# Hybrid SSD and Gated DeltaNet block: sums of squares of k from the diagonal of kq, another order of a unit's last steps, gate loads one ahead, wider quads in the FFN

## The chip, the cores and the metric

The kernel runs on one core of a Trainium2 chip. The metric is the device time of one execution in microseconds (us). TensorE (PE) multiplies, VectorE (DVE), ScalarE (ACT) and GpSimd (POOL) work on tiles, and SyncE (SP) issues the loads.

## The reference

One decoder block on 256 tokens of width 2048: a Mamba-2 mixer (SSD, 8 groups) and a Gated DeltaNet mixer (GDN, 16 qk heads, 32 v heads of 128) side by side, merged by sigmoid gates, then w_o, then a SwiGLU FFN (hidden 5632), with RMS norms and shift, scale and gate from a condition vector. Around the change stand the GDN normalisation and the merge:

```python
q = l2_normalize(q.reshape(bsz, seq, GDN_N_QK_HEADS, Dk)) * (Dk ** -0.5)
k = l2_normalize(k.reshape(bsz, seq, GDN_N_QK_HEADS, Dk))
...
a_mat = jnp.where(strict, jnp.einsum('bhcld,bhcsd->bhcls', kc, kc) * dec * bc[..., None], 0.0)
...
qk = jnp.einsum('bhcld,bhcsd->bhcls', qc, kc) * dec
...
o = rms_norm(o, norm_w) * jax.nn.silu(z.astype(f32).reshape(bsz, seq, H, Dv))
...
merged = jax.nn.sigmoid(gate_ssm) * y_ssm + jax.nn.sigmoid(gate_gdn) * y_gdn
```

l2_normalize divides by the root of the sum of squares plus 1e-6. The products of k with k hold these sums for k on their diagonal.

## The kernel before, in words

All weights are read from HBM once, as items of 512 KB. An item is loaded on SP's queue (L144, tile raw, 5 buffers), split by ScalarE into a rounded part hi (L146) and by VectorE into the rest lo (L148, 4 buffers each), and used by 24 products of 128x256 on TensorE (hi by x hi, hi by x lo, lo by x hi: L221 to L223; the form with two tiles of four blocks, quad_items, L243 to L245). pump() (L155) takes one item: it loads ahead up to LA + 1 = 4 items, issues the products, runs what is due behind earlier ones (posts), and then advances a generator by one step. A generator yields how many pumps go by until its next step, times a pace (RG for the GDN units, R_S for the SSM groups). So the mixing work is strung between the weight items, and every engine works off its instructions in the order in which pump() wrote them. SP's queue too is in order: a load that waits holds back those behind it.

The GDN mixer is eight units hu of 4 v heads and 2 qk heads, gdn_mix(hu) (L715), whose 256 tokens are two chunks c of 128. At its end a unit already works on the next one's head (gdn_head, L647): seg_rhs and seg_exp (L573, L580) for the decays E; squares (L666) and ssq (L673, one-column products with ones) for the sums of squares of q and k; rsqrt (L200 to L206, two operations on VectorE and twelve on GpSimd) to r8; kq (L686, L688) for k by k and q by k under masks, km and qm; scales for rb and bp on GpSimd (L697); and n_tile (L705) for N = E bp km. Its own steps are then: E times qm (L759), transposes of k and v, QT (transposes of E, L793), an inverse of N by blocks through DRAM (Tp L802, Tm L807, tv L814), v0, S and o0 (L864 to L880), ks and qs (L887, L893), v1 (L925), o1 (L934), norm of o (var L908 to L910 and rsqrt), gated (fo L916, o L919) and emit (the transposes ot, L943, and yh, yl). PSUM has three banks for the items' sums (plin) and five (pmx) that all tiles of the mixing steps share in turn.

Each unit's output goes through its projection w_gp, whose result proj_items adds to accg (L591). After the last unit gate_g_post (L977) multiplies accg by a gate, which was stored in DRAM and is loaded again as ggt (gg_load, L973, two buffers), in eight blocks pr, two ahead: that is the handover to the SSM groups. In the FFN the inputs h2h and h2l are made in 16 tiles (L1264 to L1267), and after tiles 4, 8 and 12 (t = 5, 9, 13) three items run, one for each of the three first accumulators, which so far need four tiles more each time.

Of the kernel before, what the change touches and what calls it, by code (L numbers as in the profile page):

```python
# [37 lines left out]
RG = [1.0] * 7 + [0.9]  # L38
# [7 lines left out]
DG = [0] + [1] * 7  # L46
# [28 lines left out]
def block_kernel(ctx: ExitStack, tc: tile.TileContext, xT, cvec, vec, dskip, consts,  # L75
# [154 lines left out]
    def quad_items(src, n, xh, xl, done, sync=False):  # L230
        bank_of = {}

        def mk(q, j):
            def mm(hi, lo):
                ah, al = xh(), xl()
                if q == 0:
                    bank_of[j] = plin.tile([P, 2, S], F32, tag="lin", name="ps_lin")
# [410 lines left out]
    def gdn_head(hu, unit):  # L648
# [7 lines left out]
        def seg_in(c):  # L656
            rhs.append(seg_rhs(gp, sl, c, 96 + h0, ("T", "T") if c == 0 else ("N", "N")))
# [5 lines left out]
        def squares():  # L663
            for i in range(2):
                sq.append(gp.tile([P, 2, S], F32, tag="T", name="sq", bufs=2))
                A.activation(sq[i], unit["qkv"][:, 2 * i:2 * i + 2, :], AF.Square)  # L666

        def ssq():
            bs_ = bank("ssq")
            for j in range(4):  # L670
                for c in range(2):
                    i = c * 4 + j
                    T_.matmul(bs_[:, 0, i:i + 1], sq[j // 2][:, j % 2, CS[c]], ones[:, 0:1], start=True, stop=True)  # L673
            a8 = gsm.tile([P, 8], F32, tag="a8", name="a8")
            V.tensor_scalar(a8, bs_[:, 0, 0:8], EPS, None, ADD)
            hd["r8"] = rsqrt(gsm, a8, 8, "r8")

        def kq():
            qT, kT = unit["qkv"][:, 0:2, :], unit["qkv"][:, 2:4, :]
            for c in range(2):  # L680
# [4 lines left out]
                km.append(gp.tile([P, 2, P], F32, tag="W", name="km", bufs=2))  # L685
                V.tensor_tensor(km[c], b[:, 0:2, :], mid(nsl, 2), MUL)  # L686
# [26 lines left out]
        return seg_in, seg_out, squares, ssq, kq, scales, n_tile, store  # L713

    def gdn_mix(hu, units):  # L715
        unit = units[hu]
        nxt = units[hu + 1] if hu + 1 < NHU else None
        if hu == 0:
# [4 lines left out]
            seg_in, seg_out, squares, ssq, kq, scales, n_tile, store = gdn_head(hu, unit)  # L723
            seg_in(0)
            yield 1
            seg_out(0)
            seg_in(1)
            yield 1
            squares()
            seg_out(1)  # L730
            kq()
            yield 1
            ssq()
# [14 lines left out]
        nx = gdn_head(hu + 1, nxt) if nxt is not None else [lambda *a: None] * 8  # L748
        seg_in, seg_out, squares, ssq, kq, scales, n_tile, store = nx
# [32 lines left out]
        for j in range(1, 15):  # L782
# [5 lines left out]
            G.tensor_tensor(G3[:, j + 1:16, 0:j], G3[:, j + 1:16, 0:j], t3, ADD)  # L788
        QT = []
# [7 lines left out]
        yield Y_SUB[hu]  # L797
# [72 lines left out]
        A.copy(v0, b)  # L870
        seg_in(0)
# [11 lines left out]
        seg_out(0)  # L883
# [29 lines left out]
        def gated(c, ro):  # L913
# [4 lines left out]
            for h in range(4):  # L918
                V.scalar_tensor_tensor(o[c][:, h, :], o[c][:, h, :], fo[:, h:h + 1],  # L919
                                       zs[:, c, h * P:h * P + P], MUL, MUL)  # L920
        square(0)
        yield 1
# [6 lines left out]
        squares()  # L929
        seg_in(1)  # L930
# [6 lines left out]
        seg_out(1)  # L937
# [9 lines left out]
        gated(0, ro0)  # L947
        ro1 = norm(1)
        ssq()
        yield 1  # L950
        emit(0)
        kq()
        yield 1
        gated(1, ro1)
        scales()
# [21 lines left out]
    def gate_g_post(pr):  # L977
        def f(ps):
            dst = accg[:, 2 * pr:2 * pr + 2, :]
            V.scalar_tensor_tensor(dst, gg_of[pr], 1.0, dst, ADD, MUL)  # L980
            if pr + 2 < 8:
                gg_load(pr + 2)
        return [f]
# [119 lines left out]
    for g in range(NG):  # L1103
        gens.append((ssm_mix(g, unit[NHU + g]), mark + DS, R_S if g < 7 else 1.0))
        if g + 1 < NG:
            gg = [lambda: None] * 5 + [lambda: gg_load(0), lambda: gg_load(1), lambda: None]
# [124 lines left out]
    quad_items(w_gu, 3, lambda: F_["h"], lambda: F_["l"], ffn_post)  # L1231
    for j in range(3, FT):
# [17 lines left out]
    with tc.tile_pool(name="ff", bufs=1) as ff:  # L1250
# [7 lines left out]
        for t in range(KT + 1):  # L1258
            if t in (5, 9, 13):
                for _ in range(3):  # L1260
# [32 lines left out]
def _layout(inp):  # L1293
# [65 lines left out]
    def qtiles(w):  # L1359
        wq = w[:, :768].reshape(4, 4, P, 3, 2, P).transpose(3, 0, 2, 4, 1, 5).reshape(3, 4, P, 1024)  # L1360
        return np.concatenate([wq, tiles(w[:, 768:]).reshape(-1, 4, P, 1024)])

    a["w_o"] = qtiles(f["w_o"][0])
    gu = f["w_gate_up"][0].reshape(D, 2, FT, P).transpose(0, 2, 1, 3).reshape(D, 2 * FT * P)
    a["w_gu"] = qtiles(gu)
# [26 lines left out]
```

## Time and profile before

| what | us |
|---|---|
| median of 3 runs | 2792.67 (2792.53 to 2794.1) |
| the profiled execution | 2796.09 |
| its span | 2794.3 |
| TensorE busy | 2681.2 (96%) |
| VectorE busy | 1884.6 (67%) |
| ScalarE busy | 1370.3 (49%) |
| GpSimd busy | 308.1 (11%) |

The mean granted clock of TensorE is 0.985 of full speed. The GDN units run from about 270 to 1290, the handover to the SSM from about 1290 to 1345, the FFN from about 2045. A busy share is a mean over stages; what a stage is limited by is read from its own stretch.

### The profile page before, as it was taken

What the parts mean: (1) busy time and instruction counts of PE and PEld (TensorE: products, weight loads), DVE (VectorE), ACT (ScalarE), POOL (GpSimd) and SP (SyncE); (2) the same over time, 40 slices, a digit from 0 to 9 for tenths busy, and PEclk for the clock granted to TensorE, in tenths of its full rate; (3) what the DMA queues carried; (4) which work ended last, traced back from release to release, by engine and by line L of the source; (5) the groups of instructions that cost most, each with busy time, mean ns of one, the idle gap of its engine ahead of it and who ended that gap; (6) DMA issues with size and microseconds to landing.
All of it is one profiled execution on the core that took longest, in us unless ns stands there. A gap on an engine that the chain in (4) does not pass through costs nothing.

```text
span 2794.3 us, 51759 instructions
## 1 busy us (share of the span) xinstructions
PE 2681.2 (96%) x20930; PEld 2550.3 (91%) x20930; DVE 1884.6 (67%) x2794; ACT 1370.3 (49%) x2250; POOL 308.1 (11%) x684
## 2 busy tenths in 40 slices
PE   6999999999999999998899999999989999999998
PEld 5988898999899998897799989999989999999997
DVE  7777657668587686766667767677666666655444
ACT  3335554655455555454565565664444444444442
POOL 0000312403123041310000000002100000000000
PEclk8999999999999999998899999999999999999999
DMA  8886647556474664743555544546656666655553
GB/s 331 317 313 212 199 161 242 177 197 227 145 251 158 215 201 165 237 144 127 189 185 193 172 160 159 174 166 238 239 173 227 226 226 226 228 200 196 194 195 130
DMA packets 183283, 566.90 MB, mean 203 GB/s; under 512 B 34753, under 2 KB 43777, under 8 KB 183041
## 3 DMA queue, kind: packets, MB, share of 16 engines
q1 hardware_dynamic: 154306, 552.56, 57.9%
q10 hardware_dynamic: 28736, 11.01, 1.5%
q8 instruction: 164, 2.69, 0.4%
q14 instruction: 77, 0.63, 0.1%
HBM read 552.49 MB, written 11.01 MB: 202 GB/s over the span
## 4 chain that ended last, share of the span: by engine, by line
PE 65%; issue 15%; DVE 7%; ACT 5%; POOL 4%; DMA 4%; SPq 0%; ACTq 0%; DVEq 0%; POOLq 0%
PE ps_lin L221 14%; PE ps_lin L223 14%; PE ps_lin L222 14%; PE ps_z L267 3%; PE ps_z L269 3%; PE ps_z L268 3%; DVE lo L148 2%; ACT hi L146 2%; DMA araw<-in_w_ada 1%; DMA raw<-in_w_g 1%; PE td L837 1%; PE tw L829 1%; PE ps_q L405 1%; DVE araw L333 1%; PE ps_lin L245 1%
## 5 line engine op out<-in xcount | busy, mean ns | idle before, releaser
L148 DVE TENSOR_TENSOR lo<-raw,hi 128x1024 fp32r<-128x1024 f32 x825 | 1014.3, 1234 | 723.4 <-ACT hi L146 721.5
L146 ACT CAST hi<-raw 128x1024 fp32r<-128x1024 f32 x825 | 860.5, 1050 | 597.2 <-PE ps_lin L222 287.3
L221 PE MATMUL ps_lin<-hh,hi 128*128 128x256 f32 x1792 | 509.5, 284 | 6.7 <-DVE accg L591 6.7
L223 PE MATMUL ps_lin<-hh,lo 128*128 128x256 f32 x1792 | 500.8, 279 | 0.6 <-DVE lo L148 0.6
L222 PE MATMUL ps_lin<-hl,hi 128*128 128x256 f32 x1792 | 500.9, 280 | 0.0
L221 PE MATMUL ps_lin<-h2h,hi 128*128 128x256 f32 x1312 | 362.1, 276 | 0.0
L222 PE MATMUL ps_lin<-h2l,hi 128*128 128x256 f32 x1312 | 362.1, 276 | 0.0
L223 PE MATMUL ps_lin<-h2h,lo 128*128 128x256 f32 x1312 | 362.1, 276 | 0.0
L221 PEld LDWEIGHTS ps_lin<-hh,hi 128*128 128x128 f32 x1792 | 340.9, 190 | 10.8 <-issue 9.3
L222 PEld LDWEIGHTS ps_lin<-hl,hi 128*128 128x128 f32 x1792 | 341.8, 191 | 3.6 <-issue 2.4
L223 PEld LDWEIGHTS ps_lin<-hh,lo 128*128 128x128 f32 x1792 | 340.4, 190 | 0.8 <-DVE lo L148 0.8
L221 PE MATMUL ps_lin<-yh,hi 128*128 128x256 f32 x896 | 259.9, 290 | 13.3 <-DVE accg L591 11.9
L222 PE MATMUL ps_lin<-yl,hi 128*128 128x256 f32 x896 | 253.4, 283 | 0.0
L223 PE MATMUL ps_lin<-yh,lo 128*128 128x256 f32 x896 | 253.3, 283 | 0.0
L221 PEld LDWEIGHTS ps_lin<-h2h,hi 128*128 128x128 f32 x1312 | 246.3, 188 | 0.0
L222 PEld LDWEIGHTS ps_lin<-h2l,hi 128*128 128x128 f32 x1312 | 246.3, 188 | 0.0
L223 PEld LDWEIGHTS ps_lin<-h2h,lo 128*128 128x128 f32 x1312 | 246.3, 188 | 0.0
L267 PE MATMUL ps_z<-hi,hh 128*128 128x512 f32 x512 | 207.7, 406 | 0.0
L269 PE MATMUL ps_z<-hi,hl 128*128 128x512 f32 x512 | 201.5, 393 | 0.0
L268 PE MATMUL ps_z<-lo,hh 128*128 128x512 f32 x512 | 200.5, 392 | 0.0
L223 PE MATMUL ps_lin<-fh,lo 128*128 128x256 f32 x704 | 194.3, 276 | 0.0
L221 PE MATMUL ps_lin<-fh,hi 128*128 128x256 f32 x704 | 194.3, 276 | 0.0
(328 smaller groups left out, 5295.6 us busy)
## 6 DMA issues: line engine op xcount, KB each, us to landing
raw<-in_w_gu SPq DMA_DIRECT2D x176, 512.0 KB, 4.2
raw<-in_w_g SPq DMA_DIRECT2D x143, 512.0 KB, 4.4
raw<-in_w_ada SPq DMA_DIRECT2D x128, 512.0 KB, 5.0
raw<-in_w_s SPq DMA_DIRECT2D x96, 512.0 KB, 3.8
raw<-in_w_dn SPq DMA_DIRECT2D x88, 512.0 KB, 4.2
araw<-in_w_ada SPq DMA_DIRECT2D x64, 512.0 KB, 7.6
raw<-in_w_gz SPq DMA_DIRECT2D x64, 512.0 KB, 4.5
raw<-in_w_gp SPq DMA_DIRECT2D x64, 512.0 KB, 4.2
```

The costliest lines, as they stand in the source:

```text
L146: A.copy(hi, raw)
L148: V.tensor_sub(lo, raw, hi.bitcast(F32))
L221: T_.matmul(ps[:, t, :], hi[:, s], h_, start=kt == 0, stop=False)
L222: T_.matmul(ps[:, t, :], hi[:, s], al[:, kt, :], start=False, stop=False)
L223: T_.matmul(ps[:, t, :], lo[:, s], h_, start=False, stop=kt == nk - 1)
L245: T_.matmul(ps[:, t, :], hi[:, s], al[:, kt, :], start=False, stop=False)
L267: T_.matmul(pss[c], hh[:, kt, cs], hi[:, s], start=kt == 0, stop=False)
L268: T_.matmul(pss[c], hh[:, kt, cs], lo[:, s], start=False, stop=False)
L269: T_.matmul(pss[c], hl[:, kt, cs], hi[:, s], start=False, stop=kt == KT - 1)
L333: V.scalar_tensor_tensor(raw, raw, 0.5, cact[:, hs], MUL, MUL, accum_out=ada2[:, j, hf:hf + 1])
L405: T_.matmul(ps[:, t, :], hi[:, s], x1[:, kt, :], start=first, stop=last)
L829: T_.matmul(b[:, h, :], N[c][:, h, :], Vo(c, bs)[:, h], start=True, stop=True)
```

## The change

Four things change.

1. Sums of squares. squares() makes only q's, and ssq() four one-column products instead of eight. For k four scalar_tensor_tensor per unit multiply the k by k tile with the identity and sum the row into the accumulator, which is written to a8. kq is called from ssq, so its products, the diagonals and the masks move from the unit's last steps to the step of S and o0.
2. Order of a unit's last steps. Besides, seg_out(0) and scales go to the step of ks and qs, gated(0) to that of o1, seg_in(1) and seg_out(1) to later ones, and the two transposes QT one pump later with one pump less behind them. Unit 0's generator begins one pump later (DG), unit 7's pace is 0.95 instead of 0.9 (RG).
3. Handover. The load of gate block pr + 1 is issued ahead of the product of block pr, in place of the load of pr + 2 behind it; one load is issued at the start instead of two.
4. FFN. w_gate_up's first six pairs of columns (3 before) are laid out as quads; the last three accumulators come from pmx, and six items run at t = 5, 9 and 13.

```diff
-RG = [1.0] * 7 + [0.9]
+RG = [1.0] * 7 + [0.95]
 R_M = 1.2
...
 NPER = 4
-DG = [0] + [1] * 7
+DG = [1] * 8
 DS = 1
...
                 if q == 0:
-                    bank_of[j] = plin.tile([P, 2, S], F32, tag="lin", name="ps_lin")
+                    bank_of[j] = plin.tile([P, 2, S], F32, tag="lin", name="ps_lin") if j < 3 else \
+                        bank("ps_lin", (P, 2, S))
                 ps = bank_of[j]
...
         def seg_in(c):
-            rhs.append(seg_rhs(gp, sl, c, 96 + h0, ("T", "T") if c == 0 else ("N", "N")))
+            rhs.append(seg_rhs(gp, sl, c, 96 + h0, ("N", "N") if c == 0 else ("T", "T")))
...
         def squares():
-            for i in range(2):
-                sq.append(gp.tile([P, 2, S], F32, tag="T", name="sq", bufs=2))
-                A.activation(sq[i], unit["qkv"][:, 2 * i:2 * i + 2, :], AF.Square)
+            sq.append(gp.tile([P, 2, S], F32, tag="T", name="sq", bufs=2))
+            A.activation(sq[0], unit["qkv"][:, 0:2, :], AF.Square)
         def ssq():
+
             bs_ = bank("ssq")
-            for j in range(4):
+            for j in range(2):
                 for c in range(2):
-                    i = c * 4 + j
-                    T_.matmul(bs_[:, 0, i:i + 1], sq[j // 2][:, j % 2, CS[c]], ones[:, 0:1], start=True, stop=True)
-            a8 = gsm.tile([P, 8], F32, tag="a8", name="a8")
-            V.tensor_scalar(a8, bs_[:, 0, 0:8], EPS, None, ADD)
-            hd["r8"] = rsqrt(gsm, a8, 8, "r8")
-
-        def kq():
+                    T_.matmul(bs_[:, 0, 2 * c + j:2 * c + j + 1], sq[0][:, j, CS[c]], ones[:, 0:1],
+                              start=True, stop=True)
+            a8 = gsm.tile([P, 2, 4], F32, tag="a8", name="a8")
+            kq(a8)
+            V.tensor_scalar(a8[:, :, 0:2], bs_[:, 0, 0:4].rearrange("p (c j) -> p c j", j=2), EPS, None, ADD)
+            V.tensor_scalar(a8[:, :, 2:4], a8[:, :, 2:4], EPS, None, ADD)
+            hd["r8"] = rsqrt(gsm, a8.rearrange("p c j -> p (c j)"), 8, "r8")
+
+        def kq(a8):
             qT, kT = unit["qkv"][:, 0:2, :], unit["qkv"][:, 2:4, :]
...
                 km.append(gp.tile([P, 2, P], F32, tag="W", name="km", bufs=2))
+                for j in range(2):
+                    V.scalar_tensor_tensor(km[c][:, j, :], b[:, j, :], 1.0, ident, MUL, MUL,
+                                           accum_out=a8[:, c, 2 + j:3 + j])
                 V.tensor_tensor(km[c], b[:, 0:2, :], mid(nsl, 2), MUL)
...
             nc.sync.dma_start(pools["i16"], consts[0:64, C_I16:C_I16 + 256])
-            seg_in, seg_out, squares, ssq, kq, scales, n_tile, store = gdn_head(hu, unit)
+            seg_in, seg_out, squares, ssq, scales, n_tile, store = gdn_head(hu, unit)
+            squares()
             seg_in(0)
             yield 1
+            ssq()
             seg_out(0)
+            yield 1
             seg_in(1)
             yield 1
-            squares()
             seg_out(1)
-            kq()
-            yield 1
-            ssq()
             yield 1
...
             G.tensor_tensor(G3[:, j + 1:16, 0:j], G3[:, j + 1:16, 0:j], t3, ADD)
+        yield 1
         QT = []
...
             QT.append(QTc)
-        yield Y_SUB[hu]
+        yield Y_SUB[hu] - 1
         gd = dr.tile([64 * 256], F32, tag="gd", name="gd")
...
         A.copy(v0, b)
+        squares()
         seg_in(0)
...
         A.copy(o[0], b)
-        seg_out(0)
+        ssq()
         yield 1
...
                                        zs[:, c, h * P:h * P + P], MUL, MUL)
+        seg_out(0)
         square(0)
+        scales()
         yield 1
...
         ro0 = norm(0)
-        squares()
-        seg_in(1)
         yield 1
...
         square(1)
-        seg_out(1)
+        gated(0, ro0)
         ogh, ogl = y_tiles(hu)
...
         yield 1
-        gated(0, ro0)
         ro1 = norm(1)
-        ssq()
+        seg_in(1)
         yield 1
         emit(0)
-        kq()
+        seg_out(1)
         yield 1
         gated(1, ro1)
-        scales()
         n_tile(0)
...
         def f(ps):
+            if pr + 1 < 8:
+                gg_load(pr + 1)
             dst = accg[:, 2 * pr:2 * pr + 2, :]
             V.scalar_tensor_tensor(dst, gg_of[pr], 1.0, dst, ADD, MUL)
-            if pr + 2 < 8:
-                gg_load(pr + 2)
         return [f]
...
         if g + 1 < NG:
-            gg = [lambda: None] * 5 + [lambda: gg_load(0), lambda: gg_load(1), lambda: None]
+            gg = [lambda: None] * 6 + [lambda: gg_load(0), lambda: None]
             unit.append(s_in(g + 1, G0 + NHU + g, gg if g == 0 else None))
...
-    quad_items(w_gu, 3, lambda: F_["h"], lambda: F_["l"], ffn_post)
-    for j in range(3, FT):
+    quad_items(w_gu, 6, lambda: F_["h"], lambda: F_["l"], ffn_post)
+    for j in range(6, FT):
         lin_items([w_gu[j, b] for b in range(4)], lambda: F_["h"], lambda: F_["l"], KT, ffn_post(j))
...
             if t in (5, 9, 13):
-                for _ in range(3):
+                for _ in range(6):
                     pump()
...
```

Three places show what moves; rows are in each engine's order of issue.

The end of a GDN unit on VectorE before, in the step with ssq and the next one with kq (a8's row is L675, lo and accg belong to the weight items, yl to the output):

```order
L201 TENSOR_SCALAR roy<-roy 128x4
L675 TENSOR_SCALAR a_8158<-ssq 128x8
L200 TENSOR_SCALAR r8y<-a_8158 128x8
L201 TENSOR_SCALAR r8y<-r8y 128x8
L148 TENSOR_TENSOR lo<-raw,hi 128x1024
L591 TENSOR_TENSOR accg<-ps_lin,accg 128x512
L945 SCALAR_TENSOR_TENSOR yl<-ot,vs,yh 128x4x128
L686 TENSOR_TENSOR km<-kq,cst 128x256
L688 TENSOR_TENSOR qm<-kq,cst 128x256
L686 TENSOR_TENSOR km<-kq,cst 128x256
L688 TENSOR_TENSOR qm<-kq,cst 128x256
```

And VectorE now, in the step of S and o0, some six steps earlier in the unit:

```order
L148 TENSOR_TENSOR lo<-raw,hi 128x1024
L592 TENSOR_TENSOR accg<-ps_lin,accg 128x512
L690 SCALAR_TENSOR_TENSOR km,a_7949<-kq,cst 128x128 x2
L692 TENSOR_TENSOR km<-kq,cst 128x256
L694 TENSOR_TENSOR qm<-kq,cst 128x256
L690 SCALAR_TENSOR_TENSOR km,a_7949<-kq,cst 128x128 x2
L692 TENSOR_TENSOR km<-kq,cst 128x256
L694 TENSOR_TENSOR qm<-kq,cst 128x256
L677 TENSOR_SCALAR a_7949<-ssq 128x2x2
L678 TENSOR_SCALAR a_7949<-a_7949 128x2x2
L200 TENSOR_SCALAR r8y<-a_7949 128x8
L201 TENSOR_SCALAR r8y<-r8y 128x8
```

The four km, qm rows now stand behind vt, with the diagonals (L690, two rows of two) ahead of the masks, and r8's two operations close the group.

VectorE from the step of v1 on before (var and roy are the norm of c = 0, fo and o its gates):

```order
L200 TENSOR_SCALAR roy<-var 128x4
L201 TENSOR_SCALAR roy<-roy 128x4
L148 TENSOR_TENSOR lo<-raw,hi 128x1024
L591 TENSOR_TENSOR accg<-ps_lin,accg 128x512
L935 TENSOR_TENSOR o_7900<-o_8070,o_7900 128x512
L148 TENSOR_TENSOR lo<-raw,hi 128x1024
L591 TENSOR_TENSOR accg<-ps_lin,accg 128x512
L916 SCALAR_TENSOR_TENSOR fo<-roy,rq 128x4
L919 SCALAR_TENSOR_TENSOR o_7899<-o_7899,fo,zs 128x128 x4
```

And now:

```order
L200 TENSOR_SCALAR roy<-var 128x4
L201 TENSOR_SCALAR roy<-roy 128x4
L148 TENSOR_TENSOR lo<-raw,hi 128x1024
L592 TENSOR_TENSOR accg<-ps_lin,accg 128x512
L942 TENSOR_TENSOR o_7942<-o_8152,o_7942 128x512
L923 SCALAR_TENSOR_TENSOR fo<-roy,rq 128x4
L926 SCALAR_TENSOR_TENSOR o_7941<-o_7941,fo,zs 128x128 x4
L148 TENSOR_TENSOR lo<-raw,hi 128x1024
L592 TENSOR_TENSOR accg<-ps_lin,accg 128x512
```

fo and the four products of o stand ahead of a lo and an accg that they stood behind.

SP's queue at the handover before (w_gp is the last unit's projection, w_s the first SSM group's input):

```order
L144 DMA raw<-in_w_gp 128x1024 x2
L975 DMA ggt<-ggd 128x512 x2
L144 DMA raw<-in_w_gp 128x1024 x2
L975 DMA ggt<-ggd 128x512
L144 DMA raw<-in_w_gp 128x1024
L975 DMA ggt<-ggd 128x512
L144 DMA raw<-in_w_gp 128x1024
L975 DMA ggt<-ggd 128x512
L144 DMA raw<-in_w_gp 128x1024
L975 DMA ggt<-ggd 128x512
L144 DMA raw<-in_w_s 128x1024
```

And now:

```order
L144 DMA raw<-in_w_gp 128x1024 x3
L980 DMA ggt<-ggd 128x512
L144 DMA raw<-in_w_gp 128x1024 x2
L980 DMA ggt<-ggd 128x512
L144 DMA raw<-in_w_gp 128x1024
L980 DMA ggt<-ggd 128x512
L144 DMA raw<-in_w_gp 128x1024
L980 DMA ggt<-ggd 128x512
L144 DMA raw<-in_w_gp 128x1024
L980 DMA ggt<-ggd 128x512
L144 DMA raw<-in_w_s 128x1024
```

The first two loads of ggt come apart, and that of block 2, the first that has to wait for a buffer, stands behind six blocks of w_gp instead of four.

## Rows read from the trace of the kernel before

**Rows 1.** Stretches: a unit, and the handover; us, busy by engine, PEclk, DMA, GB/s.

```profile
893.00:1010.00 117.00, 114.12 (x882) 106.47 (x881) 86.10 (x148) 60.42 (x114) 30.40 (x70) 1.00 0.60 199
...
1290.00:1345.00 55.00, 34.47 (x208) 32.87 (x207) 21.95 (x36) 13.18 (x22) 3.72 (x12) 0.77 0.24 82
...
1345.00:1350.00 5.00, 5.00 (x25) 5.00 (x25) 0.86 (x3) 0.00 (x0) 0.00 (x0) 0.50 0.59 202
```

**Rows 2.** TensorE's waits, units 0 to 7 (270 to 1255): total us, times, longest.

```profile
PE qt L793 <- DVE E L759: 11.1, 8, 1.8
PE tv L814 <- DVE Tm L807: 7.1, 3, 3.7
PE ot L943 <- DVE o L919: 7.1, 7, 1.2
PE seg L580 <- ACT T L573: 4.7, 1, 4.7
```

**Rows 3.** Timeline of TensorE at a unit's end: start, us, instruction, [idle before].

```profile
744.51 0.28 PE L221 MATMUL ps_lin<-yh,hi 128*128 128x256 f32 x1
...
747.33 1.84 PE L673 MATMUL ssq<-ones,sq 128*128 128x1 f32 x16
749.04 0.36 PE L221 MATMUL ps_lin<-yh,hi 128*128 128x256 f32 x1
```

**Rows 4.** VectorE's waits, units 0 to 7 (270 to 1255).

```profile
DVE N L705 <- POOL bp L697: 17.8, 8, 3.5
```

**Rows 5.** Timeline of GpSimd in the same steps, first, slowest and last of twelve.

```profile
742.92 0.20 POOL L203 TENSOR_TENSOR rot<-roy 128x4 f32<-128x4 f32 x1 [65.16 <-DVE roy L201]
...
745.18 1.19 POOL L203 TENSOR_TENSOR rot<-roy 128x4 f32<-128x4 f32 x1
...
747.02 0.20 POOL L206 TENSOR_TENSOR roy<-roy,rot 128x4 f32<-128x4 f32 x1
```

**Rows 6.** Timeline of VectorE in the same steps.

```profile
752.70 1.14 DVE L919 SCALAR_TENSOR_TENSOR o<-o,fo,zs 128x128 f32<-128x128 f32 x4
...
754.63 0.16 DVE L675 TENSOR_SCALAR a<-ssq 128x8 f32<-128x8 f32 x1
...
757.54 0.41 DVE L686 TENSOR_TENSOR km<-kq,cst 128x256 f32<-128x256 f32 x1
```

**Rows 7.** TensorE's waits in unit 7 alone (1130 to 1255).

```profile
PE tv L814 <- DVE Tm L807: 1.8, 1, 1.8
```

**Rows 8.** Waits at the handover (1285 to 1350): SP's queue, then TensorE.

```profile
SPq L975 <- DVE accg L980: 52.3, 6, 11.9
...
PE ps_lin L221 <- DVE accg L591: 18.6, 5, 6.7
```

**Rows 9.** Timelines at the handover: VectorE, SP's queue, ScalarE, VectorE, SP's queue.

```profile
1298.72 0.69 DVE L980 SCALAR_TENSOR_TENSOR accg<-ggt,accg 128x512 f32<-128x512 f32 x1
...
1299.44 0.33 SPq L975 DMA_DIRECT2D ggt<-ggd  x1
1299.87 0.37 SPq L144 DMA_DIRECT2D raw<-in_w_gp  x1
...
1304.14 1.04 ACT L146 CAST hi<-raw 128x1024 fp32r<-128x1024 f32 x1 [8.23 <-DMA raw<-in_w_gp]
...
1305.22 1.23 DVE L148 TENSOR_TENSOR lo<-raw,hi 128x1024 fp32r<-128x1024 f32 x1 [5.80 <-ACT hi L146]
1306.36 0.69 DVE L591 TENSOR_TENSOR accg<-ps_lin,accg 128x512 f32<-128x512 f32 x1
...
1307.80 0.33 SPq L975 DMA_DIRECT2D ggt<-ggd  x1
```

**Rows 10.** Groups by line and form: count, busy us, mean ns, idle before.

```profile
L333 DVE DVE_READ_ACCUMULATOR raw<-raw,cact 128x1 f32 x128 | 10.4, 81 | 0.0
```

**Rows 11.** Timelines in the FFN's start: ScalarE, then VectorE.

```profile
2059.93 1.05 ACT L146 CAST hi<-raw 128x1024 fp32r<-128x1024 f32 x1 [1.68 <-PE ps_lin L245]
...
2062.16 0.48 DVE L1264 SCALAR_TENSOR_TENSOR htmp<-accs,wsf,rf 128x256 f32<-128x256 f32 x1
```

More of the change, by code (lines that the diff above doesn't have):

```diff
@@ L712, in store @@
                         .rearrange("h (p s) -> p h s", s=P), hd["N"][c])
-        return seg_in, seg_out, squares, ssq, kq, scales, n_tile, store
+        return seg_in, seg_out, squares, ssq, scales, n_tile, store
     def gdn_mix(hu, units):
@@ L747, in gdn_mix @@
         CS = [slice(0, P), slice(P, S)]
-        nx = gdn_head(hu + 1, nxt) if nxt is not None else [lambda *a: None] * 8
-        seg_in, seg_out, squares, ssq, kq, scales, n_tile, store = nx
+        nx = gdn_head(hu + 1, nxt) if nxt is not None else [lambda *a: None] * 7
+        seg_in, seg_out, squares, ssq, scales, n_tile, store = nx
         eg = ecum[:, 96 + h0:100 + h0]
@@ L1358, in _layout, with qtiles @@
     a["w_sp"] = ptiles(f["w_ssm_proj"][0])
[L1359 to L1363, printed above, removed]
+    def qtiles(w, n):
+        wq = w[:, :256 * n].reshape(4, 4, P, n, 2, P).transpose(3, 0, 2, 4, 1, 5).reshape(n, 4, P, 1024)
+        return np.concatenate([wq, tiles(w[:, 256 * n:]).reshape(-1, 4, P, 1024)])
+    a["w_o"] = qtiles(f["w_o"][0], 3)
     gu = f["w_gate_up"][0].reshape(D, 2, FT, P).transpose(0, 2, 1, 3).reshape(D, 2 * FT * P)
-    a["w_gu"] = qtiles(gu)
+    a["w_gu"] = qtiles(gu, 6)
     wd = f["w_down"][0].reshape(FT, P, 16, P).transpose(2, 0, 1, 3).reshape(8, 11, BLK, P, P)
```

## The prediction, made before the changed kernel ran

> **What bounds the kernel now.** I read the table of stretches first, then TensorE's waits, then the instructions around those waits. In a GDN unit TensorE is busy 114.12 of 117 us while VectorE has 86.10 and ScalarE 60.42 [rows 1]: TensorE sets the pace, and only what takes work or a wait from it counts. The exception is the handover from GDN to SSM: from 1290 to 1345 TensorE is busy 34.47 of 55 us at a granted clock of 0.77, from 1345 to 1350 at 0.50 (the level 1.2 GHz), and no engine is full there [rows 1]. So there are two places to look at: the waits inside the eight units, and the handover.
>
> Inside the units TensorE's waits are few: the QT transposes for the products E (11.1 us in 8 waits, none over 1.8), the transposes tv for Tm (7.1 in 3), the output transposes ot for o (7.1 in 7), and once 4.7 us for seg at the start of unit 0 [rows 2]. An item of weights takes TensorE about 2.8 us (from 744.51 to 747.33 in rows 3): this is what one pump is worth.
>
> **The sum, against the profiled execution (2796.1 us, 3.4 above the median of 2792.67).** A measurement of this kernel can tell about 0.2%, 5.6 us, from no change.
>
> *Sums of squares.* The eight one-column products (16 instructions) hold TensorE from 747.33 to the next item at 749.04, 1.71 us [rows 3]. Half of them go, in 8 units: 8 x 0.85 = **-6.8**. The other end is a gain of nothing, if the wait that stands beside them comes back elsewhere. The Trainium skill (TensorE: Matmul & The Clock Gate, Back-to-back issue gap) gives about 60 cycles at 2.4 GHz, 25 ns, for a product of up to 64 columns; by that figure 64 removed instructions would be worth an estimated 1.6 us. Here 16 took 1.71 us, 107 ns each, and the measured row decides. The eight products of kq are only moved. ScalarE loses one of a unit's two Squares, which is off the path: ScalarE has 57 us idle in a unit.
>
> *QT one pump later.* The four products E run on VectorE behind the four N of the step before; N itself waits on GpSimd for bp, 17.8 us in 8 waits [rows 4]. The extra pump moves the QT transposes 2.8 us later on TensorE, more than the longest wait of 1.8, and with the sums of squares a few steps earlier bp is ready long before N. So the whole wait goes: **-11** (lower end -6, if N, now one step later for c=1, delays E by about what bp's wait did). The pump is taken from the yields behind it, so tv comes at the same item as before.
>
> *Gates of c=0 one pump earlier.* The rsqrt chain of GpSimd runs from 742.92 to 747.22, twelve operations; one beside a lo takes 1.19 us instead of 0.20 [rows 5]. On VectorE the four gate products come at 752.70, behind a lo and an add, and end at 753.84 [rows 6]; a wait of ot is 7.1 / 7 = 1.0 us on average [rows 2], so TensorE was there about 752.8. In the new order they stand right behind the o add of the step before, some 5 us earlier, just about when the chain ends; ssq's time before ot has gone too. I take **-6** of the 7.1; the ends are -7 and 0. By the Trainium skill (SBUF — State Buffer, the section on two separate sides) an operation of VectorE with two SBUF inputs and one of GpSimd that reads SBUF lock each other out for a whole instruction; the 1.19 agrees, and by that rule a second such meeting would put 1 us back into each ot. The margin is a rival below, not a term.
>
> *Pace of unit 7, 0.9 to 0.95.* Its steps spread a little, and tv there waits 1.8 us for Tm [rows 7]: **-1.5** (between -1.8 and 0). The other tv waits are those of units 0 and 1 and stay.
>
> *Unit 0.* Its generator starts one pump later, so that ScalarE has one item more to make seg's right side; 4.7 us wait there now [rows 2]. **-3** (0 to -5).
>
> *Handover.* SP waits 52.3 us in 6 waits for the product of an earlier block before it issues the next load of gg, and TensorE 18.6 us in 5 for accg [rows 8]. The chain: the product at 1298.72 ends, SP issues ggt at 1299.44 and only behind it the raw weights at 1299.87; ScalarE's cast comes at 1304.14 after 8.23 idle on that DMA, VectorE's lo at 1305.22, the add to accg at 1306.36 with the next product right behind it, and SP's next ggt at 1307.80 [rows 9]. That is one turn of 8.36 us for one item, against 2.8 of TensorE. In the new order ggt of block pr+1 is issued ahead of the product of block pr and waits only on that of pr-1: the same turn now serves two items. Product 5 (counted from 0) comes before at 1299.4 + 5 x 8.36 = 1341, and now at about 1302 (product 1, at TensorE's pace) + 2 x 8.36 = 1319: 22 us earlier. From the stretch at clock 0.50 another 2.5 can come back. **-25**; the ends are -15 (if product 1 is as late as now) and -28.
>
> *New in the S step.* VectorE now does the diagonals and the masks together: four scalar_tensor_tensor (four took 1.14 [rows 6]) with four reads of the accumulator at 0.08 [rows 10], four masks at 0.41 and four small ones at 0.16 [rows 6]: 1.14 + 0.32 + 1.64 + 0.64 = 3.7 us, of which 1.6 is new and the rest moved. VectorE's spare time in a unit, 117 - 86.10 = 31 us, covers it as work. But the tile bank of ssq and the two of kq are free only behind it, and S, o0, ssq and both kq take all five banks of that pool. The next step takes S's and o0's for ks and qs, and seg needs ssq's. TensorE gets there one item (2.8) and the four products of ks and qs (0.5 at the pace of an item's 24) later, so it waits some 0.4 us in seven units: **+3**. Ends: 0, and +10 if a lo and an add (1.23 and 0.69) stand ahead of the burst.
>
> *More w_ada halves per unit in GDN, fewer in early SSM.* One more piece of VectorE work per unit, inside the same 31 us: 0.
>
> *Wider quads in the FFN.* The first h2 tiles wait behind a lo whose hi buffer TensorE holds: the cast at 2059.93 stood 1.68 us idle behind TensorE, and h2 starts only at 2062.16 [rows 11]. That is the case with three accumulators, and with six the last lo of a group waits in the same way; groups of six only put more items between two groups of tiles. 0; the end on the good side is -5.
>
> Sum: -6.8 - 11 - 6 - 1.5 - 3 - 25 + 3 = -50.3. 2796.1 - 50 = 2746, and 3.4 less against the median: **2743**.
>
> **The rivals.**
> A. *The handover moves instead of going.* Product pr now needs a ggt requested only one item ahead; if that load comes in late, TensorE waits for accg as before. For: 4.3 of the 8.36 us are the raw load's way from its issue to the cast, and a ggt takes the same way. Against: ggt goes ahead of the raw in the queue. Handover worth 5 in place of 25: 2763. Chance 0.12.
> B. *More than I count.* No wait for seg's bank (3), the FFN's 5 and a full clock through the handover (3) and unit 0 (2): 2743 - 13 = 2730. Chance 0.15.
> C. *The gates meet GpSimd.* The chain of 4.3 us has one pump of 2.8 and the o add ahead of the gates; with a second collision the gates wait on it, VectorE stands, and ot's 6 stays, with half of QT's: 2743 + 6 + 5 = 2754. Chance 0.10.
> D. *Slower: the five banks.* TensorE runs in order; if VectorE reaches the burst behind a lo and an add, seg waits 3.7 + 1.23 + 0.69 = 5.6 us in each of seven units (39), and if TensorE's clock falls to 0.50 after each stop as it stands at 1345 [rows 1], an item takes 2.8 more (20): +59 against 50 won, less the 3 counted: 2743 + 56 = 2799. It decides from about 7 us a unit on. Against: TensorE stands at full clock in a unit, with 1.00 through waits of 1.8 [rows 1, 2]. Chance 0.04.
> E. *The change does not do what it says:* the sums of squares are replaced but the waits of QT and ot only trade places with the burst's: 2743 + 11 + 6 = 2760. Chance 0.07.
>
> **How the numbers follow.** The forecast has 0.52. Its own ends (handover -15 to -28, QT -6 to -11, seg 0 to +10) reach from 2737 to 2760 in part; with B on the one side and A, C and E on the other the range is 2725 to 2764, and what lies outside is D, some of A and the mishaps. Faster by over 0.2%: all but D and a remainder for what I don't see, 0.93; within 0.2%: 0.03; slower: 0.04.
>
> **What would show it.** TensorE's waits from 270 to 1255: no line of QT for E, ot below 2 us in all, and seg at most 4 us in seven waits. N no longer waiting for GpSimd. The stretch of 55 us before the first SSM item at 2.8 us an item, about 30, with SP's waits for ggt at half or less. FFN: the waits for h2 unchanged at 3 to 4 us. It would be wrong if seg or the v1 products appeared with several us each, if accg's waits were still 18 us, or if the clock in the units fell under 0.95.

## The result, and the profile after

The changed kernel is faster: 2772.63 us median against 2794.1, ratio 0.9879 (95% interval 0.9839 to 0.9919), 1.2% where the prediction had 1.8%. The single executions tell more than the median. Of eleven, the changed kernel has four from 2743.8 to 2754.4 and seven from 2772.3 to 2779.8; the kernel before has nine from 2790.9 to 2802.8 and two at 2818.7 and 2819.8. Between two groups of one kernel lie some 26 us, and between the like groups of the two kernels some 45. The profiled execution, 2779.77 us, is one of the upper group; that of before, 2796.09, one of the lower. Their stages, from the start of the first instruction named to the next, in us (kn is a unit's first transpose, yt the transposes of an SSM group's output, in two steps a group):

| stretch | before | after |
|---|---|---|
| start to unit 0's kn | 297.6 | 302.4 |
| unit 0's kn to unit 7's | 824.9 | 804.0 |
| unit 7's kn to the third yt step (the second SSM group's first) | 299.0 | 271.4 |
| from there to the first product of h2h | 629.5 | 630.0 |
| first h2h to first fh (FFN, first part) | 488.7 | 506.1 |
| first fh to the end of the last product | 242.4 | 251.7 |

The units and the handover give 48 us; the FFN, which was to stay as it is, takes 27 back. The 4.8 us more at the start are no effect: in the runs of the changed kernel and its variants unit 0's kn comes at anything from 296.6 to 302.8.

TensorE's waits in the units (270 to 1255), after; total, times, longest:

```profile
PE ot L950 <- DVE o L926: 9.3, 7, 6.6
PE tv L820 <- DVE Tm L813: 3.6, 1, 3.6
PE ssq L673 <- ACT sq L666: 3.0, 1, 3.0
PE seg L582 <- DVE var L915: 2.5, 5, 0.5
PE seg L582 <- ACT rl L574: 0.7, 1, 0.7
PE seg L582 <- ACT T L574: 0.2, 1, 0.2
```

The line of QT for E is gone [rows 2], tv is halved, unit 0's seg has become a shorter wait of ssq. ot has not fallen (7.1 before): 6.6 of its 9.3 are one wait in unit 7, around which the granted clock falls too, to 0.66 from 1210 to 1220.

VectorE's waits, same stretch:

```profile
DVE fo L923 <- POOL roy L206: 25.2, 16, 2.3
...
DVE N L711 <- POOL bp L703: 1.2, 1, 1.2
```

N hardly waits for GpSimd any more (17.8 in 8 before [rows 4]); now the gates do, at each fo (2.0 us at c = 0 and 0.9 at c = 1 in most units).

The handover after, waits from 1240 to 1310 of SP's queue and of TensorE:

```profile
SPq L980 <- DVE accg L987: 27.5, 6, 10.4
...
PE ps_lin L221 <- DVE accg L592: 3.8, 4, 1.4
```

And its stretch (columns as in [rows 1]):

```profile
1275.00:1300.00 25.00, 22.60 (x194) 21.95 (x192) 17.35 (x26) 10.63 (x16) 5.00 (x12) 1.00 0.38 131
```

SP's waits for ggt are half of [rows 8], TensorE's wait for accg a fifth, and the clock stays at 1.00 where it was 0.77 and 0.50 [rows 1]. The sixth product of accg and gate before, and the first and the sixth after:

```profile
1345.18 0.68 DVE L980 SCALAR_TENSOR_TENSOR accg<-ggt,accg 128x512 f32<-128x512 f32 x1
```

```profile
1281.19 0.69 DVE L987 SCALAR_TENSOR_TENSOR accg<-ggt,accg 128x512 f32<-128x512 f32 x1
...
1303.01 0.68 DVE L987 SCALAR_TENSOR_TENSOR accg<-ggt,accg 128x512 f32<-128x512 f32 x1
```

Before, the first came at 1298.72 [rows 9]: from the first to the sixth it took 46.5 us, and now takes 21.8.

A long stretch of the FFN, before and then after, without a single wait of TensorE in either:

```profile
2100.00:2750.00 650.00, 650.00 (x5737) 650.00 (x5737) 373.33 (x423) 281.98 (x334) 6.47 (x5) 1.00 0.63 213
```

```profile
2100.00:2700.00 600.00, 600.00 (x5097) 600.00 (x5096) 330.63 (x377) 250.81 (x298) 5.17 (x4) 1.00 0.60 205
```

650 / 5737 is 113.3 ns a product, 600 / 5097 is 117.7, at the same granted clock of 1.00 and with no more load on the other engines and on the DMAs. **This is what the prediction did not know of: a run of weight items goes at one of two paces, 113 or 118 ns a product.** In the two traces I cut TensorE's work at everything that is not a product of an item at one of the two paces: 383 runs of 15 or more are left, and each keeps one pace from about its fifth product to its end. Before, 23% of the products in them are at 118, after 72%. In the stretch from 270 to 1290 it is 1205 products before and 3107 after: 1902 x 4.4 ns = 8 us that the units gave back.

Where that comes from is seen behind QT in one unit. TensorE's timeline before, with its wait for E:

```profile
889.38 1.35 PE L793 MATMUL qt<-cst,E 128*128 128x128 f32 x8 [1.78 <-DVE E L759]
...
891.04 0.28 PE L222 MATMUL ps_lin<-hl,hi 128*128 128x256 f32 x1
...
892.17 0.28 PE L223 MATMUL ps_lin<-hh,lo 128*128 128x256 f32 x1
```

And after, without the wait:

```profile
880.82 1.04 PE L799 MATMUL qt<-cst,E 128*128 128x128 f32 x8
...
882.16 0.28 PE L222 MATMUL ps_lin<-hl,hi 128*128 128x256 f32 x1
...
883.34 0.28 PE L223 MATMUL ps_lin<-hh,lo 128*128 128x256 f32 x1
```

The two products shown are ten apart: 1.13 us before, 1.18 after. Before, the run behind QT is at 113 in units 1 to 7; after, at 118 in all seven. A run of 288 products at 4.4 ns more costs 1.3 us, about the whole wait that went (11.1 us in 8).

That the wait sets the pace is not shown. Over all traces, units 1 to 7, it holds for most but not for all: of 21 runs behind a wait of QT one is at 118, and of 57 behind QT without a wait and without an added product two are at 113. The one at 118, in the run of the kernel before with the new handover:

```profile
534.09 1.36 PE L808 MATMUL qt<-cst,E 128*128 128x128 f32 x8 [0.76 <-DVE E L774]
...
535.52 0.28 PE L238 MATMUL ps_lin<-hh,lo 128*128 128x256 f32 x1
...
536.70 0.28 PE L236 MATMUL ps_lin<-hh,hi 128*128 128x256 f32 x1
```

Ten products in 1.18 us.

### The profile page after: what moved, and what is told of

It is laid out like the page before. It is cut to its first block, busy times and chain, and to the rows that moved or that the text cites. A ratio compares the mean times of both kernels' runs of the same rounds, so it can differ in the third digit from the quotient of the medians.

```text
span 2778.0 us, 51708 instructions
## 1 busy us (share of the span) xinstructions
PE 2693.8 (97%) x20866; PEld 2572.7 (93%) x20866; DVE 1894.1 (68%) x2866; ACT 1367.3 (49%) x2242; POOL 316.9 (11%) x684
## 4 chain that ended last, share of the span: by engine, by line
PE 66%; issue 21%; DVE 5%; POOL 3%; ACT 2%; DMA 2%; SPq 0%; DVEq 0%; POOLq 0%; ACTq 0%
PE ps_lin L221 14%; PE ps_lin L223 14%; PE ps_lin L222 14%; PE ps_z L268 2%; PE ps_z L269 2%; PE ps_z L270 2%; DVE lo L148 1%; DMA araw<-in_w_ada 1%; PE ps_q L406 1%; PE ps_lin L246 1%; PE ps_lin L247 1%; PE ps_lin L245 1%; PE td L843 1%; PE tw L835 1%; DVE araw L334 1%
## 5 line engine op out<-in xcount | busy, mean ns | idle before, releaser
L221 PE MATMUL ps_lin<-h2h,hi 128*128 128x256 f32 x1216 | 341.7, 281 | 0.0
L222 PE MATMUL ps_lin<-h2l,hi 128*128 128x256 f32 x1216 | 341.7, 281 | 0.0
L223 PE MATMUL ps_lin<-h2h,lo 128*128 128x256 f32 x1216 | 341.7, 281 | 0.0
L222 PEld LDWEIGHTS ps_lin<-h2l,hi 128*128 128x128 f32 x1216 | 233.5, 192 | 0.0
L221 PEld LDWEIGHTS ps_lin<-h2h,hi 128*128 128x128 f32 x1216 | 228.3, 188 | 0.0
L223 PEld LDWEIGHTS ps_lin<-h2h,lo 128*128 128x128 f32 x1216 | 228.3, 188 | 0.0
L222 PE MATMUL ps_lin<-fl,hi 128*128 128x256 f32 x704 | 197.8, 281 | 0.0
```

The lines of the kernel that those rows point to most:

```text
L221: T_.matmul(ps[:, t, :], hi[:, s], h_, start=kt == 0, stop=False)
L222: T_.matmul(ps[:, t, :], hi[:, s], al[:, kt, :], start=False, stop=False)
L223: T_.matmul(ps[:, t, :], lo[:, s], h_, start=False, stop=kt == nk - 1)
```

## The experiments

Theory A: the prediction's terms hold, and a run's pace is set by how it starts and kept until something else runs on TensorE. The rivals: single terms have another cause, or the pace belongs to the execution, or to what runs beside it. For stretches the table's marks are used, because they can be compared whatever pace the FFN has; a unit is taken from its first kn to the next unit's. Where no number of executions is given, it is one.

**Handover undone.**

```diff
-            if pr + 1 < 8:
-                gg_load(pr + 1)
             dst = accg[:, 2 * pr:2 * pr + 2, :]
             V.scalar_tensor_tensor(dst, gg_of[pr], 1.0, dst, ADD, MUL)
+            if pr + 2 < 8:
+                gg_load(pr + 2)
...
-            gg = [lambda: None] * 6 + [lambda: gg_load(0), lambda: None]
+            gg = [lambda: None] * 5 + [lambda: gg_load(0), lambda: gg_load(1), lambda: None]
```

> The changed kernel with the gate loads of the handover as before (two ahead, issued behind the product). Theory A (the handover's gain is the prediction's 25): the stretch from unit 7's kn to the SSM's third output step gets 22 to 28 us longer than in the changed kernel, TensorE waits 15 to 20 us for accg again and the clock falls to about 0.8 there. Theory B (the handover came right by the other edits, which let unit 7 end earlier): under 8 us.

2798.89 us. Waits of SP's queue (1240 to 1340) and of TensorE (1250 to 1330):

```profile
SPq L980 <- DVE accg L985: 53.1, 6, 14.6
...
PE ps_lin L221 <- DVE accg L592: 15.8, 5, 4.1
```

And the handover's stretch:

```profile
1270.00:1325.00 55.00, 36.94 (x235) 35.73 (x234) 20.48 (x33) 11.95 (x20) 3.64 (x12) 0.78 0.32 101
```

Unit 7's kn to the third yt takes 294.2 instead of 271.4: 22.8 us, with SP's waits and the low clock back. Theory A.

**The handover alone, in the kernel before.** The same edit the other way round, in the kernel before, with the two products of the FFN told of below.

> The kernel before with the FFN's two products and the handover of the changed kernel alone. Theory A (the handover's gain is its own): the stretch from unit 7's kn to the SSM's third output step, 299 us before, falls by 22 to 26. Theory B (it needs the other edits): by less than 15.

The stretch falls from 299.1 to 273.5, 25.6 us (2774.13 us in all). The term stands by itself.

**k's sums by products with ones again**, in the new order:

```diff
-            sq.append(gp.tile([P, 2, S], F32, tag="T", name="sq", bufs=2))
-            A.activation(sq[0], unit["qkv"][:, 0:2, :], AF.Square)
+            for i in range(2):
+                sq.append(gp.tile([P, 2, S], F32, tag="T", name="sq", bufs=2))
+                A.activation(sq[i], unit["qkv"][:, 2 * i:2 * i + 2, :], AF.Square)
...
-            for j in range(2):
+            for j in range(4):
                 for c in range(2):
-                    T_.matmul(bs_[:, 0, 2 * c + j:2 * c + j + 1], sq[0][:, j, CS[c]], ones[:, 0:1],
-                              start=True, stop=True)
+                    i = c * 4 + j
+                    T_.matmul(bs_[:, 0, i:i + 1], sq[j // 2][:, j % 2, CS[c]], ones[:, 0:1], start=True, stop=True)
...
-                for j in range(2):
-                    V.scalar_tensor_tensor(km[c][:, j, :], b[:, j, :], 1.0, ident, MUL, MUL,
-                                           accum_out=a8[:, c, 2 + j:3 + j])
```

> The changed kernel with k's sums of squares made by one-column products with ones again (all eight, two Squares), everything else in the new order. Theory A (prediction): a unit gets 0.85 us longer by TensorE's work and the 0.5 us of seg's wait for its bank gets shorter or goes, as the diagonals no longer stand ahead in VectorE: net 0.4 to 0.9 us a unit, 116.0 to 116.4 to 116.9. Theory B (the products are hidden or nearly free, 25 ns each): 116.0 to 116.2 or less, or even shorter by the seg wait.

Units 2 to 6 take 116.8 to 117.0, where the changed kernel has 116.0 (2748.86 us, with the FFN at 113). 0.85 us a unit for eight instructions is the row's 107 ns each: theory A for the products. The 25 ns that the Trainium skill has (TensorE: Matmul & The Clock Gate, Back-to-back issue gap) do not hold for them here. seg's five waits of 0.5 stay as they are, so the diagonals don't cause them.

**Without the extra pump ahead of QT:**

```diff
-        yield 1
         QT = []
...
-        yield Y_SUB[hu] - 1
+        yield Y_SUB[hu]
```

> The changed kernel without the extra pump ahead of the QT transposes (the yield behind them as before). Theory A (prediction: the pump gives the 11 us): QT waits again for E, 1 to 1.8 us in each unit; and as it then starts behind a wait, the run behind QT takes 113, as in the kernel before, and gives back 1.3 us a unit: units of about 116. Theory B (the wait went because bp is ready earlier, N no longer waiting for GpSimd): no wait at QT, pace 118, units 116.0 as they are.

Theory B. TensorE's waits in the units, whole answer down to 1 us:

```profile
PE ot L949 <- DVE o L925: 9.4, 6, 6.6
PE ssq L673 <- ACT sq L666: 3.2, 1, 3.2
PE seg L582 <- DVE var L914: 2.5, 5, 0.5
PE tv L819 <- DVE Tm L812: 2.2, 1, 2.2
PE tw L834 <- ACT Vm L820: 1.8, 1, 1.8
```

No QT, pace 118 behind it, units 2 to 6 of 116.1 (but for one of 119.8, in which a tw, a product of the inverse of N, waited). The pump was not needed for the wait to go. VectorE's wait for bp is gone in this run too, which speaks for the earlier bp; but the new order moves other steps of VectorE as well, and none was moved back alone. What the pump would do without the earlier bp was not tried.

**Gates of c = 0 late again** (with the FFN's two products):

```diff
         square(1)
-        gated(0, ro0)
         ogh, ogl = y_tiles(hu)
...
         yield 1
+        gated(0, ro0)
         ro1 = norm(1)
```

> The changed kernel with the FFN's two products, and with the gates of c = 0 one step later, as before. Theory A (prediction: the earlier gates are worth 6 of ot's 7.1): TensorE waits about 0.8 us more a unit at ot of c = 0, units of 116.8. Theory B (with ssq's products gone from the step ahead and less work on VectorE there, ot of c = 0 finds o ready anyway): units stay at 116.0.

```profile
PE ot L964 <- DVE o L941: 15.7, 14, 6.5
```

6.4 us more of waiting than the 9.3 of the changed kernel (9.2 with the FFN's products), 14 waits in place of 7: 1.1 at c = 0 in each of units 2 to 6. Units 4 to 6 take 117.1, 116.8 and 115.7, with 403, 333 and 93 products at 118; with the early gates and the FFN's products the same units take 116.0, 116.2 and 116.0, with 381, 451 and 333. At equal pace the early gates are worth 0.8 to 1.2 us a unit. Theory A. Units 2 and 3 took 120 and 122, as a tw waited there for Vm (4.1 us in 2 waits) and the clock fell to 0.99 and 0.97; such waits come in single units of several of the runs. 2763.1 us in all.

**Unit 7's pace at 0.9.** One number changed.

> The changed kernel with the pace of unit 7 back at 0.9. Theory A (the pace term was mis-sized: with 0.95 the unit's last steps outrun the weight items, and TensorE stands 6.6 us for ot with nothing else to do): that wait falls to about 1 us or less, tv's wait in unit 7 comes back with about 1.8 us, and the time from unit 7's first transposes (kn) to the second SSM output step falls by some 4 us. Theory B (the 6.6 us comes from GpSimd's chain for c = 1, whatever the pace): ot's wait in unit 7 stays above 5 us. The whole time can't tell them apart, as the FFN's pace moves it by 26 us; the stretch does.

Neither theory as written: ot's longest wait is 4.4, a wait of 4.8 for accg comes behind it, and tv does not wait in unit 7 at 0.9 either. The second SSM output step, the expectation's mark, comes 186.7 us after unit 7's kn, 2.8 sooner than in the changed kernel (189.6); the third, the table's mark, after 273.7, 2.2 later. But runs at 0.95 with the changed handover and no added product behind QT in unit 7 lie from 188.1 to 189.6 and from 269.6 to 272.5 on these marks, so either difference is little more than their spread (2749.5 us in all, with the FFN at 113). The changed kernel's 6.6, on TensorE and then on GpSimd and VectorE:

```profile
1207.57 0.60 PE L950 MATMUL ot<-cst,o 128*128 128x128 f32 x4
1214.77 1.17 PE L950 MATMUL ot<-cst,o 128*128 128x128 f32 x4 [6.60 <-DVE o L926]
...
1208.86 1.14 POOL L203 TENSOR_TENSOR rot<-roy 128x4 f32<-128x4 f32 x1 [3.47 <-DVE roy L201]
...
1210.64 1.15 POOL L206 TENSOR_TENSOR roy<-roy,rot 128x4 f32<-128x4 f32 x1
...
1213.84 0.20 POOL L206 TENSOR_TENSOR roy<-roy,rot 128x4 f32<-128x4 f32 x1
...
1214.07 0.16 DVE L923 SCALAR_TENSOR_TENSOR fo<-roy,rq 128x4 f32<-128x4 f32 x1 [2.34 <-POOL roy L206]
```

Between the two ot there is no weight item: they have run out, and the chain of norm, GpSimd and gates of c = 1 shows bare. Two of GpSimd's twelve operations in it start beside a lo and take 1.14 and 1.15 us, the others 0.20.

**Other starts of a run.** Small products, whose result nobody uses, one kind per unit behind QT, and in the FFN every eight items by turns (the copy of one column frees the bank):

```diff
+    def kick(kind, m, r):
+        b = bank("kick")
+        if kind == "c":
+            T_.matmul(b[:, 0, 0:1], m, ones[:, 0:1], start=True, stop=True)
+        elif kind[:1] == "m":
+            for i in range(int(kind[1:])):
+                T_.matmul(b[:, i, :], m, m, start=True, stop=True)
+        elif kind == "r":
+            T_.matmul(b[:, 0, :], r, r, start=True, stop=True)
+        elif kind == "t":
+            T_.transpose(b[:, 0, :], m, m)
+        A.copy(kd_[0], b[:, 0, 0:1])
```

> The changed kernel with small products, whose result nobody uses, at two places: one kind per unit right behind the QT transposes (units 1 to 6: a one-column product, one 128x128 product, two, a rounded 128x128 product, a transpose, four 128x128 products; units 0 and 7 none), and one every eight items in the FFN. Theory A (a run of items takes its pace, 113 or 118 ns a product, from how it starts, and keeps it until something else runs on TensorE): in the changed kernel the runs behind QT are all at 118; here some kinds turn them to 113 and the same kind gives the same pace in the FFN, where the pace changes only at these places. Theory B (the pace belongs to the execution or to what VectorE, ScalarE and the loads do beside it): all runs behind QT stay alike, and the FFN's pace doesn't change at the places.

Three of its places: one 128x128 product behind QT (two instructions), a rounded one in the FFN, and eight items later four 128x128 products:

```profile
530.62 0.39 PE L104 MATMUL kick<-cst 128*128 128x128 f32 x2
...
530.97 0.28 PE L238 MATMUL ps_lin<-hl,hi 128*128 128x256 f32 x1
...
531.99 0.28 PE L238 MATMUL ps_lin<-hl,hi 128*128 128x256 f32 x1
```

```profile
2145.28 0.22 PE L106 MATMUL kick<-h2h 128*128 128x128 f32 x1
...
2145.51 0.28 PE L238 MATMUL ps_lin<-h2l,hi 128*128 128x256 f32 x1
...
2146.57 0.28 PE L238 MATMUL ps_lin<-h2l,hi 128*128 128x256 f32 x1
...
2168.00 1.05 PE L104 MATMUL kick<-ones 128*128 128x128 f32 x8
...
2169.02 0.28 PE L238 MATMUL ps_lin<-h2l,hi 128*128 128x256 f32 x1
...
2170.16 0.28 PE L239 MATMUL ps_lin<-h2h,lo 128*128 128x256 f32 x1
```

Nine products take 1.02 us behind the first, nine take 1.06 behind the second, ten 1.14 behind the third: 113, 118, 113. Behind QT, with one place for each kind, one column or one product gives 113, and two products, four, the rounded one and the transpose 118. The FFN's 26 places cut it into runs of mostly 192 products, and each run is at one pace from about its fifth product to its end. Behind two and behind four products it was 113 each time, entered at either pace; behind one column, always entered at 113, 118 each time; behind one product and the rounded one the other pace than before it, each time. So in the FFN the pace follows what ran last, and at which pace that was entered, and not the load beside it. The kind alone does not tell: two products give 118 behind QT and 113 in the FFN, which theory A had otherwise. Nor do kind and entry tell all: of the runs behind QT with no wait that were entered at 118, two went at 113 and the rest at 118. The whole took 2775.83 us.

**The FFN's pace fixed**, in both kernels: two products of ones behind the second item after the last h2 tile.

```diff
+        n = 0
         while items:
+            if n == 2:
+                kick("m2", ones, None)
+            n += 1
             pump()
```

> The changed kernel with two 128x128 products of ones, whose result nobody uses, once in the FFN, behind the second item after the last h2 tile. Theory A (the FFN's pace of 113 or 118 ns is set by how its long run starts, and this start gives 113, as in all eight places of the run with the kinds by turns): every execution has the FFN at 113, the executions lie together within some 10 us around 2748, and none is at 2770 to 2780. Theory B (the pace belongs to the execution, or to the wider quads): two groups 26 us apart remain, most executions above 2770.

> The kernel before with the same two products at the same place of its FFN. Theory A: all executions near 2793, none at 2819, so that the difference to the changed kernel with the same products is the change's own worth, 45 us (prediction's sum 50, less 8 for the pace behind QT and in the units). Theory B: as without them, some at 2819.

(Of the places with the kinds by turns five had two products, not eight; all five gave 113.) The changed kernel: six executions, 2745.3 to 2756.4, median 2751.14; none above. The kernel before: ten, nine of them from 2792.7 to 2805.3 with a median of 2795.99, and one at 2847.1, whose granted clock was 0.936 where the nine had 0.982 to 0.987; it is left out. Beside them the kernel before without the products had twelve of fifteen at 2820 to 2829 and three at 2795 to 2800. A stretch of the FFN of the changed kernel with the products:

```profile
2100.00:2500.00 400.00, 400.00 (x3531) 400.00 (x3531) 246.15 (x300) 175.99 (x223) 0.00 (x0) 1.00 0.69 222
```

400 / 3531 is 113.3 ns. Theory A: with the FFN at one pace in both, the change is worth 2795.99 - 2751.14 = 44.9 us.

**And one product behind QT in every unit:**

```diff
             QT.append(QTc)
+        kd = ['m1', 'm1', 'm1', 'm1', 'm1', 'm1', 'm1', 'm1'][hu]
+        if kd:
+            kick(kd, ident, triu_r)
         yield Y_SUB[hu] - 1
```

> The changed kernel with the FFN's two products and also one 128x128 product behind the QT transposes in every unit. Theory A: the 287 to 312 products behind QT run at 113 instead of 118 in all units (1.3 us a unit), less 0.35 for the product itself: 0.9 us a unit, some 7 us less than without it, about 2741. Theory B: the pace stays at 118 and the eight products cost 3 us: 2751.

2743.48 median of six (2740.3 to 2747.9): 7.7 less; units 2 to 6 take 114.9 to 115.6, and the run behind QT is at 113 in all units. Theory A. This is faster than both kernels: ratio to the kernel before 0.9737 (0.9704 to 0.977), where that one ran mostly with its FFN at 118.

**Three accumulators in the FFN's quads** (with the two products; the sizes 6 back to 3):

> The changed kernel with the FFN's two products, and with three accumulators in quads in the FFN as before. Theory A (prediction: wider quads are worth nothing): the stretch from the SSM's third output step to the first down product (1117 to 1120 us in the runs with the FFN at 113) stays within 2 us. Theory B (the six items between two groups of tiles hide the tiles): 5 us longer.

From the third yt to the first fh it is 1123.1 us, in the runs with six and the two products 1119.5, 1119.8, 1120.4 and 1120.7: some 3 us longer, between the two theories. The first part of the FFN alone is 494.5 here, and 489.6 to 493.7 with six; the kernel before, with three, has 488.7 to 490.8. With one trace of each, and 4 us between runs of one code in that part, a worth of up to some 3 us can be neither shown nor excluded; theory B's 5 us are not met.

**Unit 7's pace at 1.0**, with all the added products:

> The changed kernel with one product behind QT, two in the FFN, and the pace of unit 7 at 1.0. Theory A (unit 7's 6.6 us at ot come from its tail running past the weight items): with 1.0 the tail is one item later still, the wait grows by some 3 us and the time with it, 2746. Theory B (the pace doesn't set that wait): 2743 as with 0.95, within 2 us.

2741.5 to 2752.7 in four, median 2750.85; the longest wait of ot is 6.6 as at 0.95, and from unit 7's kn to the third yt it takes 269.2 (268.4 at 0.95). Theory B for the stretch. In the execution with a trace (2751.2) the higher time is in units 1 and 3 (118.4 and 120.7), where a tw waited as above; whether this holds for the other two near 2751 is not known.

## Why the prediction was right, and where not

**The sum.** -50 was forecast, 2743. With the FFN at one pace it is -45, and in the profiled pair, ahead of the FFN, -43; the pace in the units hides 8 more. The step that failed is the unwritten one: that a product of an item costs the same before and after. The FFN's 6,336 products (264 items of 24) at 118 in place of 113 ns would be 28 us; the table's last two lines have 27, and this, not a term of the sum, brings the median to 2772.6, above the range's upper end of 2764 (the ratio 0.9879 on the 2792.67 shown with the prediction is 2759, inside). On which side of that end the median fell was luck: it hangs on how many executions had the FFN at 118. Why the changed kernel, by its times, had it so in seven of eleven and the kernel before in two of eleven is not settled: in two later comparisons the kernel before had it so in twelve of fifteen and in three of seven. The 0.2% that the prediction took as told from no change were for that reason too fine: one kernel's executions lie 26 us apart.

Unit 4 shows how the terms of a unit add up, by the starts on TensorE. It takes 118.63 us before and 115.97 after. QT's wait and its transposes, which run faster without the wait (1.35 and 1.04 us above), are 2.1 less, ot's wait and its transposes 1.05, ssq 0.9; the seg step takes 0.35 more and the items' pace 1.1.

**Sums of squares, -6.8.** Right: 0.85 a unit where undone.

**QT, -11.** The wait went, and without the pump, which the prediction put first; the earlier bp, its second reason, fits. Some 8 of it came back as pace, since the run behind QT went at 113 with the wait and at 118 without it. With a product behind QT the units fall to 114.9 to 115.6.

**Gates, -6.** Worth 6.4 us of waiting where they are undone, some 1 us a unit. But ot's waits as a whole have risen, from 7.1 to 9.3: in the units ahead of the last they fall from about 1.0 to 0.5, and the remaining 0.5 is now at c = 1; in unit 7 ot waits 6.6, where it waited 1.8 in two. This is what I missed: with no item left, the chain of c = 1 has nothing to hide behind. Rival C came true in part: fo waits for GpSimd 2.0 us at c = 0 in a unit.

**Unit 7's pace, -1.5.** Not told from none. tv's wait in unit 7 is gone, but not by the pace: it is also gone at 0.9, and in the two other traces of the kernel before. **Unit 0, -3.** 4.7 of seg against 3.0 of ssq, 1.7; this edit was not undone by itself.

**Handover, -25.** 22.8 undone, 25.6 alone; the turn now serves two items, as worked out: from the first product of accg and gate to the sixth 46.5 us before and 21.8 now, where 41.6 and 19.6 were reckoned.

**The burst and seg's bank, +3.** Nothing. The burst after, VectorE from its first to its last, with TensorE's seg of that step:

```profile
960.62 0.28 DVE L690 SCALAR_TENSOR_TENSOR km<-kq,cst 128x128 f32<-128x128 f32 x1
960.83 0.08 DVE L690 DVE_READ_ACCUMULATOR km<-kq,cst 128x1 f32 x1
...
963.50 0.17 DVE L201 TENSOR_SCALAR r8y<-r8y 128x8 int32<-128x8 int32 x1
...
965.08 0.59 PE L581 MATMUL seg<-N,triu_r 128*128 128x512 f32 x1
```

3.05 us, as the instructions overlap, where I had 3.7; the bank of ssq is free at 963.2 and seg comes at 965.08 without a wait. Rival D never came near. That seg waits 2.5 us in all, near the 3, is luck: these are the waits of c = 1 in the step of ot, and they are gone where the gates are late.

**FFN quads, 0.** Not told from none, within some 3 us. Rivals A and B did not come true; what E feared for QT came about by the pace, not by the burst.

## What to carry to other kernels

Before a wait is priced at its length, look at the pace of the run behind it: count products per us in the long stretches without waits of both kernels. If two executions of one kernel differ by a fixed step, compare the stretch where nothing waits first; here one pair of useless products decided 26 us. And where a load stands in a queue ahead of what the engine needs next, the turn through the queue, not the transfer, is the price; asking for it one block ahead of its release halved what a block took here, from 46.5 to 21.8 us over five.

## What the runs showed that I had not expected

TensorE's products of 128x256 at full granted clock go at 113.3 or 117.7 ns with the same work beside them, and a run of more than 5,000 keeps its pace. In the traces the pace changes only where something else runs on TensorE in between; which one follows depends on the kind and on what went before, and mostly repeats from unit to unit (seven of seven behind QT in the profiled pair, either way; 75 of 78 over all traces). What in TensorE makes the two is open; no run here shows it.
